# Output gates for all tokens ahead of the recurrence, and masked scores of two head parities in turn, in the mixer of a two-block network

## The chip, the cores and the metric

The kernel runs on one core of one Trainium2 chip. The metric is the device time of one execution, in microseconds (us), as the median of several runs; less is better. TensorE (PE) multiplies matrices, and its weight loads (PEld) overlap with its products; VectorE (DVE), ScalarE (ACT) and GpSimd (POOL) do the work by elements, and SyncE (SP) issues most of the DMA.

## The reference, cut to what matters

The network has two blocks over 512 tokens of 1024 features. The first is a gated layer, an attention and a second gated layer; the second is a token mixer and a channel mixer. The change lies in the token mixer. Half of its columns go through a convolution over 31 tokens, the other half through a recurrence of 8 heads of 64, with an output gate:

```python
p_rw = p_rw + (prev - p_rw) * rwkv_mu
r, k, v, wd, ad, gd = jnp.split(p_rw, RWKV_SPLITS, axis=-1)
a = jax.nn.sigmoid(a0 + ad @ a2)
g = jax.nn.sigmoid(gd) @ g2                     # gd has 160 columns, g 512
y = wkv7_scan(rh, heads(decay), kh, vh, kk, heads(a))
y = layer_norm(y, LNX_EPS).reshape(B, T, RWKV_WIDTH) * lnx_g + lnx_b
y = (y + bonus) * g
return jnp.concatenate([u, y], axis=-1) @ w_out
```

The recurrence is S = S * w - (S kk) (a kk)^T + v k^T, read with r at each token. All is float32.

## The kernel before, in words

Activations lie with features on the 128 partitions and tokens along the free axis. Large products split float32 operands into two parts that single passes carry; the small products of the mixer run on float32 as it is, and the trace records each of these as two halves, with a weight load for each.

The mixer (`mixer`, line 952) projects first. Column blocks of the second projection go in four groups (`PH`), and the small work that hangs on them is woven between: rates and gates of the decays beside group 1, the chain to the recurrence's matrices beside group 2 (`keynorm`, `decay`, `products`, `lower`, `bonus`), and the solve of 32 by 32 blocks on VectorE beside group 3 (`solve_step`, lines 1171 and 1174). The last blocks of group 3 are `d0` and `d1`, the 128 and the 32 columns of the gate's latent; `gd_done` shifts them (lines 1047, 1048) and takes their sigmoid on ScalarE (line 1233) into the tiles `gd0` and `gd1`.

Then `scan` (line 1257) runs the recurrence by 8 chunks of 64 tokens, in rounds of two chunks, i = 0 to 3. `prep(i)` makes ready what a round needs: `load` brings the solved blocks back from DRAM, `turn` transposes keys (line 1319), `scores(i, n)` for n = 0 to 3 makes masked products of heads (below), `inverse1` and `inverse2` finish the inverses. `seq(i)` is the chain from chunk to chunk: `step1`, `step2`, `step3`, each one or two groups of products on TensorE, then a copy on ScalarE (lines 1368, 1374) or a sum and a product on VectorE (lines 1388, 1391). `post(i)` reads the outputs of the round before: `read`, then `norm1`, `norm2`, and `norm3`, which applies norm, bonus and gate. The taps of the convolution (124 of them, line 1000, VectorE) fill VectorE's gaps; the first 70 may run before the solve is done. After the taps come the convolution's mean and norm (`conv_mean`, `conv_rstd`, `conv_out`), then the output's products.

`scores(i, n)` has one bank of PSUM and four products of 64 rows each. Heads of even number lie on partitions 0 to 63, odd ones on 64 to 127; n % 2 is the parity, so that one call uses one half of the array's rows. VectorE then multiplies the bank by the masks (line 1337).

`norm3(i)` multiplies, for its 128 tokens, the gate's latent by the four column blocks of `g2`: eight products of 128 columns into one bank, alternately 128 and 32 rows deep, and VectorE takes the gate from PSUM (line 1434). The two parts of `g2` are loaded on POOL's queue at the start of `scan` (lines 1266, 1267).

The order of the work is set twice. `weave` emits lists of (cost, step) at even progress of their costs. Then the framework's planner orders each engine's instructions by that order and by when its model has them ready, and gives out tiles and banks; on the chip each engine runs its queue in that order. The program has eight PSUM banks (`bank`).

Of the kernel before, what the change touches and what calls it, by code (L numbers as in the profile page):

```python
# [19 lines left out]
P = 128  # L20
# [10 lines left out]
# order of work where the blocks of a projection and what hangs on them share the engines  # L31
# of the latents (a, b: queries, c: keys and values, l: rotary key) with S: rstd by tokens,
# C: norm of c, N and R: norm and rotation of l
LATENTS = "cSclalNaCbbR"
HOLD = 3, 2  # steps of the last of the first projection's blocks that wait for the softmax; those of its first round
# column blocks of the second projection: the first six, then those beside the rates, the chain to the
# recurrence's matrices, and the solve; t: values turned
PH = "u0 g0 w u1 g1 k0", "k1 k2 k3 r0", "r1 r2 r3 u2 g2", "v0 v1 t0 v2 t1 v3 t2 u3 t3 g3 d0 d1"
W_IN2 = [n for p in PH for n in p.split() if n[0] != "t" and n != "d1"]
EARLY = 70  # taps of the convolution before the solve is done  # L40
CUT = 0, 24, 49, 74, 99, 124  # taps by stage of the recurrence
NE = 2  # column blocks of the output begun beside the recurrence
# steps between the output and the next projection, at each half block of the first and each K tile of the second
# [4 lines left out]
# ---------------------------------------------------------------- host layout  # L48
def _cols(v, n=None):
    """A vector as columns of 128 partitions, zero padded."""  # L50
    v = np.asarray(v).reshape(-1)
    k = -(-v.size // P)
    if v.size != k * P:
        v = np.concatenate([v, np.zeros(k * P - v.size, v.dtype)])
    return v.reshape(k, P).T


def _swapped(v):
    """The halves of the last axis swapped: what a rotation takes the sine of."""
    return np.roll(v, v.shape[-1] // 2, -1)  # L60


def _wtiles(w):
    """[K, M] -> [M/128, 128 (k in tile), K/128, 128 (m in tile)]."""
    k, m = w.shape
    return np.ascontiguousarray(w.reshape(k // P, P, m // P, P).transpose(2, 1, 0, 3))


def _narrow(w):
    """[K, 32] -> [128 (k in tile), K/128 * 32]."""  # L70
    return np.ascontiguousarray(w.reshape(-1, P, 32).transpose(1, 0, 2)).reshape(P, -1)
# [43 lines left out]
def _constants():  # L115
    """Matrices that depend on shapes alone."""
# [111 lines left out]
# ---------------------------------------------------------------- order of work  # L228
def pipe(n, *stages):
    """Stages (cost, f(u)) of n units, later stages of earlier units first."""  # L230
# [9 lines left out]
def weave(*streams):  # L240
    """Emits lists of (cost, f), each in its own order, all at even progress."""
# [13 lines left out]
# ---------------------------------------------------------------- program  # L255
class Net:
# [28 lines left out]
    # ---- small things  # L285
# [12 lines left out]
    @contextmanager  # L298
    def phase(self, name, third=True):
        """A pool for a part of the program; with room for a third block of weights or without."""  # L300
        with self.tc.tile_pool(name=name, bufs=1) as p:
            self.pt = p
            self.slots = self.slots[:2] + ([(p, 2)] if third else [])
            yield p
# [18 lines left out]
    # ---- exact halves of float32 operands  # L323
    def weights(self, src, n, keep=None):
        """A block of weights [128, n] in two parts that single passes carry."""
# [15 lines left out]
    def weights_at(self, src, n, at):  # L341
        """The same in two given tiles."""
# [21 lines left out]
    def dense(self, ps, src, x, m=P):  # L364
        """ps = W^T x over the K tiles of x, W's column block at src ([128, K/128 * 128])."""
# [3 lines left out]
    def dense_steps(self, bank, src, x, after=None, m=P, split=8):  # L369
        """The same in steps of `split` K tiles; after(ps) when it is done."""  # L370
# [19 lines left out]
    def narrow_steps(self, src, x, new, after, gain=None, m=P):  # L390
        """32 columns: a fourth of the K tiles in each fourth of the array's columns, then their sums in m rows,
        the columns and those with swapped halves in turn. x(k): the terms of a K tile; gain: per feature."""
# [27 lines left out]
    def dense_halves(self, src, x, last, done, mid):  # L420
        """A dense block by halves of the tokens; done(h, ps), and pieces of other work by K tile of the second."""
# [15 lines left out]
    def group_halves(self, src, n, x, room, side, ws=(), done=None, W=6):  # L437
        """group by halves of the tokens: weights (but ws, those of the first K tiles) stay in room(k); side: other work after the K tiles of both halves."""
# [24 lines left out]
    def group(self, src, n, x):  # L463
        """n column blocks at once, K tile by K tile: for operands that x(k) makes one by one."""
# [9 lines left out]
    # ---- norms over features (partitions)  # L474
    def add_square(self, acc, x, first, gain=1.0):
        """acc += (gain * x)^2"""
# [9 lines left out]
    def rstd(self, acc, mat, r, eps=1e-6, rows=P, last=None):  # L486
        """r = -1/sqrt(mat^T (acc + last) + eps); acc is used up."""
# [7 lines left out]
    def nrsqrt(self, r, v, t, eps):  # L495
        """r = -1/sqrt(v + eps), with a Newton step behind the tables; t is scratch."""
# [8 lines left out]
    def log_exp(self):  # L505
        """Ln and Exp from one table of ScalarE."""
        self.tc.keep_in_program_order(self.nc.scalar.preload_act_table_set("natural_log_exp_and_others"))

    def gained(self, k, g):
        """x[k] * gain per feature in two parts."""  # L510
# [7 lines left out]
    # ---- first block  # L518
    def warm(self):
        """Matmuls of zeros while the first loads are on their way: the tensor engine's clock rises with use."""  # L520
# [5 lines left out]
    def first(self, k):  # L526
        """Loads a tile of the input; its gains and squares."""
# [11 lines left out]
    def swiglu(self, acc, gname, gu, down, new2=None, side=((), (), ()), start=None):  # L539
        """x += half a gated layer; side: work for the gaps of the other engines, a piece a column block."""  # L540
# [73 lines left out]
    def entry(self, acc1, acc2):  # L614
        """What the mixer's input asks for; acc1 and acc2 are the sums of x^2 and (x g')^2."""
# [3 lines left out]
        # gains with the signs that the norms (all negative) ask for  # L619
# [9 lines left out]
    def enter(self, h, k):  # L629
        """A tile of the mixer's input in two parts, half h of the tokens: x g rr + shift; x, spilled, is used up.  # L630
        Of the final norm and the next, y = x rstd(x) g', then y rstd(y), both roots in one:
        rstd(x) rstd(y) = 1/sqrt(mean((x g')^2) + eps mean(x^2) + eps^2)."""
# [17 lines left out]
    def attention(self, acc):  # L650
        nc, A = self.nc, self.A
        new = self.acc()
        with self.phase("att", False) as pa:
# [26 lines left out]
            def norm_head(src, sq, gain, out, mat):  # L680
                """out = -src * gain / rms(src) over the groups of mat; sq holds src squared."""
# [9 lines left out]
            # latents and rotary key (r is negative, so are these before their norms)  # L691
# [42 lines left out]
            def b_keys(f):  # L734
                """Of heads 2 f and 2 f + 1."""
# [23 lines left out]
            def b_query_norm(h):  # L759
                """With the rotation's two terms one above the other: against the rotated key twice."""  # L760
# [69 lines left out]
            # softmax and values, head by head  # L830
# [6 lines left out]
            def scores(u):  # L837
# [4 lines left out]
                else:  # L842
                    q, k = qka[f][rows], qka[4 + f][rows]
                    # minus the bias: at [p, f] the one for q - k = p + 384 - f
# [18 lines left out]
            def transposes(u):  # L863
                pts[u] = [tile_([P, T], f"pt{4 * (u % 2) + j}") for j in range(4)]
                # key tile j of queries i >= j
# [6 lines left out]
            def values(u):  # L872
                """Of heads u and u + 1, side by side in the columns of the array."""
# [32 lines left out]
    # ---- second block  # L906
    def modulation(self):
        """mod = silu(c) W + b as 48 columns, in pieces for the gaps of another phase."""
# [24 lines left out]
        def total(g, part=(0, 1)):  # L933
            """Sums over partitions, side by side in the columns of the array: a quarter for half a group."""
# [6 lines left out]
        def fold(p):  # L941
            """The sums of two groups as columns, and their bias."""
# [19 lines left out]
    def mixer(self, acc1, acc2, stop):  # L962
# [17 lines left out]
        with self.phase("mix", False) as pa:  # L980
# [4 lines left out]
            gd = [keep([P, T], "gd0"), keep([32, T], "gd1")]  # L985
# [4 lines left out]
            def conv(j, t):  # L990
                """A tap of the convolution over tokens."""
# [12 lines left out]
            # ------------ projections  # L1004
# [12 lines left out]
            def room(n):  # L1017
                """Two tiles for a block of weights, in what the recurrence doesn't use yet or any more."""
# [16 lines left out]
            def residual():  # L1035
                """1/rms(x), spilled."""
# [4 lines left out]
            def shifted(j, out):  # L1041
                """out = p (1 - mu) + prev mu, tile j of the recurrent columns."""
# [26 lines left out]
            def rates(i):  # L1069
                """Decay rates, tokens on partitions."""  # L1070
# [12 lines left out]
            def keynorm(f):  # L1083
                """kk = k k_k / max(|k k_k|, 1e-12) over a head."""
# [12 lines left out]
            def decay(f):  # L1097
                """Decays within a chunk: up to t, up to t - 1, and back."""
# [30 lines left out]
            def lower(f):  # L1129
                """-L (rows t, columns s) of the 16 chunks of a head pair."""  # L1130
# [19 lines left out]
            def bonus_v(f):  # L1150
                """The bonus times v, when both are there."""
# [4 lines left out]
            def solve_start():  # L1156
                """(I - B)^-1 of 32 by 32 blocks, a block a partition."""
# [47 lines left out]
            def v_turn(f):  # L1205
                """Values with a chunk's tokens on partitions."""
# [29 lines left out]

            first()
# [14 lines left out]
            weave(D_(PH[3]), solve)  # L1252
            gains, scratch = (ncg, nlg, ngt, nfg), (dB, dT, dX, dY)
            return self.scan(tile_, xt_, room, ra, kb, bv, vt, gd, pcm, cv, convs, gains, scratch, stop)

    def scan(self, tile_, xt_, room, ra, kb, bv, vt, gd, pcm, cv, convs, gains, scratch, stop):
        """The recurrence by chunks of 64 tokens, its norms and gates, the convolution, the output."""
# [7 lines left out]
        masks, g2, g2b, cen = xt_(5), xt_(6), xt_(7), tile_([P, P], "tiny")  # L1265
        nc.gpsimd.dma_start(g2, A["g2"][:P])
        nc.gpsimd.dma_start(g2b[:32], A["g2"][P:])
# [13 lines left out]
        # ------------ norm of the convolution  # L1281
# [23 lines left out]
        # ------------ recurrence  # L1305
        def load(i):
            """Inverses of the blocks of 32: the first of a chunk as it is, both transposed."""
# [7 lines left out]
        def turn(c):  # L1315
            """Keys (both kinds, one above the other) of a chunk with tokens on partitions."""
# [8 lines left out]
        def scores(i, n):  # L1325
# [336 lines left out]
```

## Time and profile before

| | us |
|---|---|
| median of 3 runs | 1731.52 (1730.7 to 1740.45) |
| span of the profiled execution | 1719.0 |
| TensorE busy in it | 1682.8 (98%) |
| VectorE busy | 1025.7 (60%) |
| ScalarE busy | 715.3 (42%) |
| GpSimd busy | 51.4 (3%) |

The profile is of one execution. Its span goes from the first instruction to the last; the device time that the runs give has some us more around it, and of the profiled execution only the span is known. Times of rows count from the start of the span. The ends of TensorE's products are modelled, so durations of neighbouring products overlap by some 0.1 us; the time that a group takes is read from its start to the start of the next.

### The profile page before, as it was taken

The numbers are of one execution on the slowest core, as the hardware profiler recorded it, in microseconds if no ns is written. First come the engines' busy times: TensorE is split into PE (matmuls) and PEld (weight loads), VectorE is DVE, ScalarE is ACT, GpSimd is POOL, SyncE is SP. The second block draws the span as 40 slices with busy tenths as digits, with TensorE's granted clock in tenths as the row PEclk, the third lists the DMA queues.
The fourth block names the chain that finished last, engine by engine and source line by source line (L and its number), as shares of the span: only waits on it lengthen the run. The fifth ranks groups of instructions, "written<-read, shape, count | busy, mean of one in ns | idle before, by whom it ended". The sixth has DMA issues, their size and how long they took to land.

```text
span 1719.0 us, 21909 instructions
## 1 busy us (share of the span) xinstructions
PE 1682.8 (98%) x8644; PEld 1360.1 (79%) x8644; DVE 1025.7 (60%) x1706; ACT 715.3 (42%) x1163; POOL 51.4 (3%) x104
## 2 busy tenths in 40 slices
PE   9999999999999999999999999999999999999997
PEld 7888888877776788778877877787869988888886
DVE  4544434347788655754455469996777776666224
ACT  5422222247678352222222344632346554444222
POOL 0000000000000100100010000000000000000000
PEclk9999999999999999999999999996989999999998
DMA  5333333342111534753364332321033223333332
GB/s 176 99 97 94 94 95 99 98 133 88 56 55 38 178 92 147 243 174 99 98 220 145 115 103 62 98 67 41 5 105 96 75 77 98 98 99 93 91 101 83
DMA packets 63864, 177.17 MB, mean 103 GB/s; under 512 B 17066, under 2 KB 19370, under 8 KB 63761
## 3 DMA queue, kind: packets, MB, share of 16 engines
q1 hardware_dynamic: 52016, 138.96, 27.0%
q0 software_dynamic: 9872, 34.71, 6.4%
q10 hardware_dynamic: 1872, 2.10, 0.4%
q8 instruction: 68, 1.11, 0.3%
q14 instruction: 36, 0.29, 0.1%
HBM read 169.19 MB, written 6.55 MB: 102 GB/s over the span
## 4 chain that ended last, share of the span: by engine, by line
PE 78%; issue 7%; DVE 7%; DMA 6%; ACT 2%; DVEq 0%; POOL 0%; ACTq 0%; SPq 0%; POOLq 0%
PE ps L321 77%; DMA ada<-in_ada_w 5%; PE ps L869 1%; DVE adas L931 1%; DVE wlo L351 1%; DVE Ts L1174 0%; DVE Tm L1171 0%; DVE acc L484 0%; DVE f L1608 0%; DVE x L1514 0%; DVE x L1609 0%; DVE x L1515 0%; DMA raw<-in_w_in2k 0%; PE ps L1319 0%; DMA x<-in_x 0%
## 5 line engine op out<-in xcount | busy, mean ns | idle before, releaser
L350 ACT CAST whi<-raw 128x1024 fp32r<-128x1024 f32 (+1 forms) x244 | 248.9, 1020 | 584.5 <-PE ps L321 431.8
L351 DVE TENSOR_TENSOR wlo<-raw,whi 128x1024 fp32r<-128x1024 f32 (+1 forms) x244 | 289.1, 1185 | 256.2 <-ACT whi L350 246.6
L321 PE MATMUL ps<-xh,whi 128*128 128x512 f32 (+1 forms) x1008 | 401.0, 399 | 1.3 <-ACT xh L514 1.3
L321 PE MATMUL ps<-xh,wlo 128*128 128x512 f32 (+1 forms) x1008 | 392.1, 389 | 4.2 <-DVE wlo L351 4.2
L321 PE MATMUL ps<-xl,whi 128*128 128x512 f32 (+1 forms) x1008 | 391.5, 388 | 0.3 <-DVE xl L515 0.3
L321 PEld LDWEIGHTS ps<-xh,whi 128*128 128x128 f32 x1008 | 189.9, 189 | 50.6 <-issue 5.8
L321 PEld LDWEIGHTS ps<-xh,wlo 128*128 128x128 f32 x1008 | 189.4, 188 | 46.5 <-DVE wlo L351 6.8
L321 PEld LDWEIGHTS ps<-xl,whi 128*128 128x128 f32 x1008 | 189.7, 188 | 43.9 <-issue 5.3
L321 PE MATMUL ps<-hh,wlo 128*128 128x512 f32 (+1 forms) x560 | 211.5, 378 | 5.8 <-DVE wlo L351 5.8
L321 PE MATMUL ps<-hh,whi 128*128 128x512 f32 (+1 forms) x560 | 212.0, 379 | 0.0
L321 PE MATMUL ps<-hl,whi 128*128 128x512 f32 (+1 forms) x560 | 211.1, 377 | 0.0
L321 PE MATMUL ps<-oh,whi 128*128 128x512 f32 (+1 forms) x360 | 134.5, 375 | 0.0
L321 PE MATMUL ps<-ol,whi 128*128 128x512 f32 (+1 forms) x360 | 134.4, 374 | 0.0
L321 PE MATMUL ps<-oh,wlo 128*128 128x512 f32 (+1 forms) x360 | 134.4, 373 | 0.0
L321 PEld LDWEIGHTS ps<-hh,wlo 128*128 128x128 f32 x560 | 106.2, 190 | 26.6 <-DVE wlo L351 7.5
L321 PEld LDWEIGHTS ps<-hh,whi 128*128 128x128 f32 x560 | 106.2, 190 | 25.0 <-issue 5.9
L321 PEld LDWEIGHTS ps<-hl,whi 128*128 128x128 f32 x560 | 106.1, 190 | 19.4
L554 DVE TENSOR_TENSOR s<-s,ps 128x512 f32<-128x512 f32 x44 | 30.1, 687 | 109.8 <-PE ps L321 109.8
L552 DVE TENSOR_TENSOR s<-ps,r 128x512 f32<-128x512 f32 x44 | 30.2, 690 | 87.4 <-PE ps L321 87.4
L321 PEld LDWEIGHTS ps<-ol,whi 128*128 128x128 f32 x360 | 68.3, 190 | 11.9
L321 PEld LDWEIGHTS ps<-oh,wlo 128*128 128x128 f32 x360 | 68.2, 189 | 12.0
L321 PEld LDWEIGHTS ps<-oh,whi 128*128 128x128 f32 x360 | 68.1, 190 | 11.8
(457 smaller groups left out, 2227.6 us busy)
## 6 DMA issues: line engine op xcount, KB each, us to landing
raw<-in_ffn_gu SPq DMA_DIRECT2D x82, 512.0 KB, 3.6
ada<-in_ada_w POOLq DMA_DIRECT2D x48, 512.0 KB, 4.6
raw<-in_up SPq DMA_DIRECT2D x38, 512.0 KB, 3.6
raw<-in_ffn_d SPq DMA_DIRECT2D x32, 512.0 KB, 3.6
raw<-in_w_in SPq DMA_DIRECT2D x27, 512.0 KB, 3.6
raw<-in_w_out SPq DMA_DIRECT2D x16, 512.0 KB, 3.8
raw<-in_down SPq DMA_DIRECT2D x16, 512.0 KB, 3.5
raw<-in_ffn_d SPq DMA_DIRECT2D x16, 384.0 KB, 3.2
```

The source lines that it names most:

```text
L321: self.nc.tensor.matmul(*a, **k)
L350: nc.scalar.copy(hi[:, :n], raw[:, :n])
L351: nc.vector.tensor_sub(lo[:, :n], raw[:, :n], hi[:, :n].bitcast(F32))
L552: nc.vector.tensor_mul(s, pg, r)
L554: nc.vector.tensor_mul(s, s, pu)
L869: nc.tensor.transpose(ps[:, i * P : (i + 1) * P], es[u, i][:, j * P : (j + 1) * P], self.c("ident"))
L931: nc.vector.scalar_tensor_tensor(st[g][q], h, sc[:, k : k + 1], st[g][q], op0=ALU.mult, op1=ALU.add)
```

## The change

The gate's products for all tokens move from `norm3` to the end of the projections: `gate_load` loads `g2` before group 3, and four steps `gate(f)`, woven behind group 3, make two products of 512 columns each into four banks. After the fourth, ScalarE copies the four banks into the tiles that held `g2` and the latent. `norm3` has no products any more and takes the gate from these tiles in SBUF; its cost for `weave` falls from 1.8 to 0.1.

`scores(i, g)` now makes two parities at once, with a bank for each, and issues their products in turn; both masks follow. Two calls of cost 1.8 replace four of 0.9.

Comments and docstrings are removed too.

```diff
-            gd = [keep([P, T], "gd0"), keep([32, T], "gd1")]
+            gd, gt = [keep([P, T], "gd0"), keep([P, T], "gd1")[:32]], []
...
+            def gate_load():
+                st["g2"] = xt_(6), xt_(7)
+                nc.gpsimd.dma_start(st["g2"][0], A["g2"][:P])
+                nc.gpsimd.dma_start(st["g2"][1][:32], A["g2"][P:])
+
+            def gate(f):
+                fs, (g2, g2b) = slice(f * P, (f + 1) * P), st["g2"]
+                st["gate", f] = ps = self.bank()
+                self.mm(ps, g2[:, fs], gd[0], start=True, stop=False)
+                self.mm(ps, g2b[:32, fs], gd[1], start=False, stop=True)
+                if f == 3:
+                    gt.extend((xt_(6), xt_(7), keep([P, T], "gd0"), keep([P, T], "gd1")))
+                    for n, t in enumerate(gt):
+                        nc.scalar.copy(t, st["gate", n])
...
-            weave(D_(PH[3]), solve)
+            gate_load()
+            weave(D_(PH[3]) + sum([item(1.7, gate, f) for f in range(4)], []), solve)
...
-        masks, g2, g2b, cen = xt_(5), xt_(6), xt_(7), tile_([P, P], "tiny")
-        nc.gpsimd.dma_start(g2, A["g2"][:P])
-        nc.gpsimd.dma_start(g2b[:32], A["g2"][P:])
+        masks, cen = xt_(5), tile_([P, P], "tiny")
...
-        def scores(i, n):
-            ps = self.bank()
-            sc = tile_([P, T], (f"s{i % 2}", f"s{2 + i % 2}", "di", "kk")[n], bufs=(1, 1, 2, 2)[n])
+        def scores(i, g):
+            ps, sc = [], []
+            for n in (2 * g, 2 * g + 1):
+                ps.append(self.bank())
+                sc.append(tile_([P, T], (f"s{i % 2}", f"s{2 + i % 2}", "di", "kk")[n], bufs=(1, 1, 2, 2)[n]))
             for m in range(2):
-                h = n % 2 + 4 * (n // 2) + 2 * m
-                f, R = h // 2, HR(h)
                 for q in range(2):
                     ct, k = slice(i * P + q * 64, i * P + q * 64 + 64), 2 * m + q
-                    o = ps[:, k * P : (k + 1) * P].rearrange("p (n t) -> p n t", n=2)
-                    self.mm(o, kb[f][R, 2 * i + q].rearrange("p n t -> p (n t)"), ra[f][R, :, ct], start=True, stop=True)
-                    st["sc", 2 * i + q, h] = sc[:, k * P : (k + 1) * P]
-            nc.vector.tensor_mul(sc, ps, masks)
+                    for n in range(2):
+                        h = n + 4 * g + 2 * m
+                        f, R = h // 2, HR(h)
+                        o = ps[n][:, k * P : (k + 1) * P].rearrange("p (n t) -> p n t", n=2)
+                        self.mm(o, kb[f][R, 2 * i + q].rearrange("p n t -> p (n t)"), ra[f][R, :, ct], start=True, stop=True)
+                        st["sc", 2 * i + q, h] = sc[n][:, k * P : (k + 1) * P]
+            for n in range(2):
+                nc.vector.tensor_mul(sc[n], ps[n], masks)
...
         def norm3(i):
             y4, ti = st["y", i], slice(i * P, (i + 1) * P)
-            pg = self.bank()
             for f in range(4):
-                fs = slice(f * P, (f + 1) * P)
-                self.mm(pg[:, fs], g2[:, fs], gd[0][:, ti], start=True, stop=False)
-                self.mm(pg[:, fs], g2b[:32, fs], gd[1][:, ti], start=False, stop=True)
-            for f in range(4):
-                fs, y = slice(f * P, (f + 1) * P), y4[:, f, :]
+                y = y4[:, f, :]
                 nc.vector.scalar_tensor_tensor(y, y, nlg[:, f : f + 1], bv[f][:, ti], op0=ALU.mult, op1=ALU.add)
-                nc.vector.scalar_tensor_tensor(y, y, self.v("lnxb", f), pg[:, fs], op0=ALU.add, op1=ALU.mult)
+                nc.vector.scalar_tensor_tensor(y, y, self.v("lnxb", f), gt[f][:, ti], op0=ALU.add, op1=ALU.mult)
                 self.halves(os_[4 + f][0][:, ti], os_[4 + f][1][:, ti], y)
...
-            + sum([item(0.9, scores, i, n) for n in range(4)], []) + item(1.7, inverse1, i) + item(1.7, inverse2, i)
+            + sum([item(1.8, scores, i, g) for g in range(2)], []) + item(1.7, inverse1, i) + item(1.7, inverse2, i)
...
-            item(1.7, read, 2 * i) + item(1.7, read, 2 * i + 1) + item(0.9, norm1, i) + item(0.9, norm2, i) + item(1.8, norm3, i)
+            item(1.7, read, 2 * i) + item(1.7, read, 2 * i + 1) + item(0.9, norm1, i) + item(0.9, norm2, i) + item(0.1, norm3, i)
```

## Rows read from the trace of the kernel before

**Rows 1.** The page: busy time by engine; the chain that ended last, by engine.

```profile
PE 1682.8 (98%) x8644; PEld 1360.1 (79%) x8644; DVE 1025.7 (60%) x1706; ACT 715.3 (42%) x1163; POOL 51.4 (3%) x104
...
PE 78%; issue 7%; DVE 7%; DMA 6%; ACT 2%; DVEq 0%; POOL 0%; ACTq 0%; SPq 0%; POOLq 0%
```

**Rows 2.** Stretches: length, busy us and instructions by engine; granted clock, DMA share, GB/s.

```profile
1164.00:1174.10 10.10, 6.53 (x78) 4.91 (x74) 9.60 (x21) 6.51 (x8) 0.00 (x0) 1.00 0.41 126
1174.10:1204.80 30.70, 30.64 (x238) 27.91 (x239) 15.39 (x24) 5.24 (x10) 0.00 (x0) 0.50 0.09 15
...
1225.30:1228.60 3.30, 3.30 (x18) 2.97 (x19) 2.65 (x5) 0.56 (x1) 0.00 (x0) 0.50 0.00 0
...
1249.20:1255.90 6.70, 6.70 (x74) 6.29 (x71) 4.99 (x12) 0.04 (x1) 0.00 (x0) 0.50 0.30 82
...
1273.10:1279.80 6.70, 6.70 (x39) 4.06 (x40) 3.01 (x11) 1.07 (x4) 1.06 (x2) 0.50 0.35 116
...
1204.80:1275.60 70.80, 69.94 (x764) 57.23 (x763) 51.84 (x95) 25.91 (x49) 2.69 (x5) 0.91 0.17 52
```

**Rows 3.** The chain in order of time: start us, us, what.

```profile
1228.00 27.84 PE ps L321 x324
...
1281.47 0.70 DVE acc L1287
...
1297.64 22.40 PE ps L321 x165
```

**Rows 4.** Timeline of TensorE, gate products and what follows: start us, us, operation.

```profile
1220.70 3.40 PE L321 MATMUL ps<-gd,x 128*128 128x128 f32 x16
1224.03 1.19 PE L321 MATMUL ps<-dpm,rf 32*32 32x32 f32 x32
...
1270.08 3.68 PE L321 MATMUL ps<-gd,x 128*128 128x128 f32 x16
1273.69 0.49 PE L321 MATMUL ps<-s,vt 128*64 128x64 f32 x4
```

**Rows 5.** Timeline of TensorE, fp32 products of 512 columns and what follows.

```profile
1284.69 3.79 PE L321 MATMUL ps<-sq,cst 128*128 128x512 f32 x8
1288.32 3.29 PE L321 MATMUL ps<-gd,x 128*128 128x128 f32 x16
```

**Rows 6.** Waits of TensorE, 1164 to 1304: us in total, times, longest.

```profile
PE ps L321 <- ACT oh L355: 3.3, 2, 2.6
PE ps L321 <- DMA dpm<-dT: 1.7, 1, 1.7
```

**Rows 7.** Groups of VectorE, 1166 to 1305: busy us, mean ns, idle before.

```profile
L1434 DVE SCALAR_TENSOR_TENSOR B<-B,vec,ps 128x128 f32<-128x128 f32 x16 | 5.1, 343 | 0.0
L1433 DVE SCALAR_TENSOR_TENSOR B<-B,col,bv 128x128 f32<-128x128 f32 x16 | 5.1, 347 | 0.0
```

**Rows 8.** Timeline of ScalarE: the gate's second sigmoid.

```profile
1169.59 0.62 ACT L1233 ACTIVATE gd<-gd 32x512 f32<-32x512 f32 x1
```

**Rows 9.** Timeline of POOL: the second load of g2.

```profile
1112.02 0.51 POOL L1267 DMA_DIRECT2D x<-in_g  x1 [3.94 <-DVE x L1123]
```

**Rows 10.** Timeline of TensorE: masked scores (ra,kb), and what follows two of them.

```profile
1166.76 2.82 PE L321 MATMUL ps<-ra,kb 64*128 64x128 f32 x32
...
1180.11 3.09 PE L321 MATMUL ps<-ra,kb 64*128 64x128 f32 x16
...
1185.03 2.07 PE L321 MATMUL ps<-ra,kb 64*128 64x128 f32 x8
...
1207.74 1.17 PE L321 MATMUL ps<-ra,kb 64*128 64x128 f32 x12
1208.84 1.14 PE L321 MATMUL ps<-x,dpm 64*64 64x64 f32 x16
...
1211.05 1.16 PE L321 MATMUL ps<-ra,kb 64*128 64x128 f32 x8
1212.13 1.16 PE L321 MATMUL ps<-vt,kbt 128*128 128x128 f32 x8
```

More of the change, by code (lines that the diff above doesn't have):

```diff
@@ L1251, in mixer, with scan @@
             weave(D_(PH[2]), chain)
-            weave(D_(PH[3]), solve)
+            gate_load()
+            weave(D_(PH[3]) + sum([item(1.7, gate, f) for f in range(4)], []), solve)
             gains, scratch = (ncg, nlg, ngt, nfg), (dB, dT, dX, dY)
-            return self.scan(tile_, xt_, room, ra, kb, bv, vt, gd, pcm, cv, convs, gains, scratch, stop)
-    def scan(self, tile_, xt_, room, ra, kb, bv, vt, gd, pcm, cv, convs, gains, scratch, stop):
+            return self.scan(tile_, xt_, room, ra, kb, bv, vt, gt, pcm, cv, convs, gains, scratch, stop)
+    def scan(self, tile_, xt_, room, ra, kb, bv, vt, gt, pcm, cv, convs, gains, scratch, stop):
         nc, A = self.nc, self.A
```

## The prediction

> **What bounds the kernel now.** I read the page first: TensorE is busy in 98% of the span and carries 78% of the chain that ended last [rows 1]. A microsecond saved there counts, if TensorE is also what ends the waits where it is saved. The change touches one stage, from the end of the second projection (1164 us) to the start of the output (1304 us). Its stretches come next [rows 2]: TensorE is busy without a gap from 1174.1 and nearly so to 1275.6, VectorE for half to three quarters of that, ScalarE and the DMA little. The second thing to see there is the granted clock: 0.50 (1.2 GHz) from 1174.1 to 1204.8, then full (2.4 GHz) but for three falls of 3.3 to 6.7 us before 1280. Third, the chain of waits [rows 3]: TensorE's products alone carry it to 1256 and, behind a weight block, to 1281.5; from there to 1297.6 it is VectorE and ScalarE, the convolution's norm, and TensorE has room beside it.
>
> **Gate products taken out of norm3.** One norm3 runs 8 fp32 products of 128 columns, recorded as 16 halves: from 1220.70 to the next product at 1224.03, 3.33 us; the third time, 1270.08 to 1273.69, 3.61 [rows 4]. There are four; the second repeats the first. Three lie before 1275 on the path: 3.33 + 3.33 + 3.61 = 10.3 us go. The fourth, at 1288.32 [rows 5], lies beside the convolution's chain, and TensorE waits behind it anyway (2.6 us until 1297.64) [rows 3, 6]: I count it at nothing; that chain is the cover, without it 3.3 us more would go. VectorE's sixteen products by the gate read SBUF instead of PSUM: the same form with all its tensors in SBUF takes 347 ns against 343 [rows 7], nothing.
>
> **Gate products added ahead of the recurrence.** Eight products of 512 columns, 16 halves. The nearest row is the convolution's norm: 8 fp32 halves of 512 columns from 1284.69 to the next product at 1288.32, 0.454 us each [rows 5], so 16 x 0.454 = 7.3 us. What lies beside it: half of the gate's latent is ready only when ScalarE's sigmoid ends at 1170.21 [rows 8]. Between 1164 and 1174.1 TensorE is busy 6.53 of 10.10 us [rows 2]; the 3.6 idle are waits for copies, masks and, the longest (1.7), for the solved blocks by DMA [rows 6]. Ready work can fill them: 7.3 - 3.6 = 3.7 us are added. The ends: 0, if the products displace later idle time too, and 7.3, if all run ahead of the inverses that could start at 1171. ScalarE's four copies (some 0.6 each, by the 128x512 sigmoid's kind of size [rows 8], 2.4 us) fall into stretches in which it is busy 6.51 of 10.10 and 5.24 of 30.70 us [rows 2]: nothing; ahead of the copy between the inverses they would cost 2.4. The two loads of g2 move forward on POOL's queue. The second went out at 1112.02 already, after a wait for the tile that VectorE frees [rows 9]; that is 52 us before they are needed now, and what stands behind them, masks and zeros, is needed in the recurrence: nothing. If they landed late, all of the 7.3 would be on the path, the upper end above.
>
> The Trainium skill says under Key Properties of "TensorEngine Tiling (Array Packing)" that a change of tiling mode drains TensorE. The old gate products alternate between 128 and 32 rows, and their halves take 0.208 us (3.33 / 16), where eight halves of the state's update, all of 128 rows, show 1.16 us, 0.145 each [rows 4, 10]. By that rule the new ones, eight products at twice the difference, would cost 8.3 instead of 7.3. The trace has the price for 128 columns only, and the sum stays with 7.3.
>
> **Masked scores of the two parities in turn.** One parity is four products, 8 halves, on 64 rows of the array. Alone it takes 1.08 us (1211.05 to 1212.13) at the full clock and 2.0 at half (1185.03, with 0.07 of modelled end) [rows 10]. Where two parities follow each other with nothing between, they run side by side: 12 halves, 4 of one parity and 8 of the next, from 1207.74 to 1208.84, 1.10 us, no longer than 8 alone [rows 10]. In turn, each pair should cost one, 1.1 us. Round 0: 32 halves in 2.8 us become 2.2, but behind them TensorE waits for the DMA: hidden. Round 1, at half clock: 3.0 for a pair in a row and twice 2.0 become 2 x 2.0, saves 3.0. Rounds 2 and 3: two parities alone (1.08 each), then 0.6 for half a parity by the row of 8, and the 1.10, in all 3.9; with 2.2 each saves 1.7. Sum 3.0 + 1.7 + 1.7 = 6.4. The ends: 0, if they don't run side by side; 8, if the two pairs of a round follow each other and overlap too. The first parity's mask now waits for both, up to 1 us; the inverses need all four masks, so no one waits for that one.
>
> **The clock.** The three falls between 1204.8 and 1280 each come within 5 us of a gate product's start (1220.7 and 1225.3; 1270.1 and 1273.1; the second repeats them) [rows 2, 4], which streams at two thirds of the rate of its neighbours. Without them I expect these falls to go: half clock for 3.3 + 6.7 us and 2.5 up to 1275.6 gives back half, 6.3 us (ends 0 and 6.3). The long one, 30.7 us, came behind the 3.6 us of idle time. With wide products in that place and the scores paired, part of it should go, between 0 and 15.3 us, half of 30.7. I take 5, a third, since the inverses on 32 rows that stood around the fall remain.
>
> **What is late next.** From 1204.8 to 1275.6 VectorE is busy 51.84 of 70.8 us [rows 2]; TensorE's part shrinks to 70.8 - 10.3 - 3.4 - 6.3 = 50.8. Two engines equally full that wait for each other don't both run without gaps. The ends: 0 us lost, if VectorE's remaining taps move into the first stretch (busy 15.39 of 30.70), and 20, if VectorE stays at today's share of 73%, which keeps the 70.8. I take 7, a third, nearer to the lower end because the taps are free to move.
>
> **Sum.** -10.3 + 3.7 - 6.4 - 6.3 - 5 + 7 = -17.3 us. The profiled span is 1719.0; the median of the three runs is 1731.52, 12.5 more, which I take as what lies around the span and leave as it is. After 1304 TensorE is the chain again [rows 3], and its weights' rooms come free from the recurrence itself, so the gain is kept: 1731.5 - 17.3 = 1714.2, say **1714**.
>
> **Rivals.** *The clock holds through the recurrence.* For it: paired scores fill both halves of the array, and the wide products stream without a break. Against: the inverses and the waits around them stay. The other 10 us of the first stretch come back: 1704. Chance 0.15.
>
> *TensorE was the cover, not the bound.* VectorE ends last nearly everywhere, 14 instead of 7 us are lost, and in the waits the clock falls as before (of the 6.3 half): about 1714 + 7 + 3 = 1724. For it: 51.8 us against 50.8. Against: from 1204.8 to 1275.6 TensorE is busy 69.94 of 70.8 us [rows 2]. Chance 0.27.
>
> *The pairs don't run side by side*, or the order of the queue parts them: the 6.4 stay, 1720.5. Against: the 12 halves. Chance 0.07.
>
> *Slower.* The gate products stand in TensorE's queue ahead of the inverses and wait there for the sigmoid, and they hold four of the program's eight banks until the last is copied, so that transposes and scores wait for banks. All from 1171 on is late by 7.3 and the 1.7 waited, 9 us. It decides if the recurrence is bound by the chain from chunk to chunk and not by TensorE, so that none of the 10.3 and 6.4 comes back; with the half clock some 10 us longer, 5 more: 1745. Chance 0.05. The Trainium skill points this way under Gotcha 1 of "TensorEngine Tiling (Array Packing)": row tiles raise the pressure on PSUM, as each needs a bank of its own. No row of before shows a wait for a bank.
>
> **How the numbers follow.** The forecast has 0.46, with a range of its own from 1706 to 1721. A measurement of this kernel can tell about 1%, 17.3 us, and the forecast lies on that line (1714.2): half of its chance (0.23) is faster, half the same. The clock's case is all faster (0.15), and so is a quarter of the lost cover's and of the pairs' (0.09). Faster 0.47, same 0.49, slower 0.04, nearly all of the last case. The range goes from 1700 (the clock's case and 4 us) to 1729 (the lost cover with 5 us more of the gate products on the path).
>
> **What would show it.** Right: no product of the gate's latent after 1185; 16 halves of 512 columns before, near 7.3 us in all; scores of 16 halves in 1.1 us; the full clock from about 1200 to the convolution's mean; waits of TensorE for ScalarE and VectorE in the recurrence, some 7 us in all. Wrong: the falls of the clock where they were, without the gate products; gate products that wait for the sigmoid with the inverses behind them; a stage that ends at 1304 as before.

## The result and the profile after

The changed kernel takes 1707.33 us (median of 4 executions, 1705.04 to 1709.47) where the kernel before, run beside it, takes 1731.11 (4 executions, 1722.40 to 1740.45): ratio 0.9854, interval [0.9814, 0.9893]. The forecast was 1714, range 1700 to 1729. In later runs, with more executions (12 and 30), it was 1706.91 against 1716.83: 0.9943 [0.9922, 0.9965]. Six of the 63 later executions of the kernel before were in a slower state: they count in its medians, but not in the ratios and the clock columns below. The changed kernel takes the same both times, the kernel before does not, and how far the runs explain this is the main thing to learn here.

The page of the changed kernel, as in [rows 1]: the span, TensorE's busy time, and the chain's shares by engine.

```profile
span 1706.2 us, 21821 instructions
PE 1662.1 (97%) x8596; PEld 1340.5 (79%) x8596; DVE 1025.2 (60%) x1706; ACT 717.3 (42%) x1167; POOL 51.4 (3%) x104
...
PE 76%; DVE 8%; issue 7%; DMA 7%; ACT 2%; POOL 0%; DVEq 0%; ACTq 0%; SPq 0%; POOLq 0%
```

This execution took 1708.19, so only 2.0 us lie around its span, and 1.7 to 2.2 in the executions below. The profiled execution of before (span 1719.0) therefore took about 1721, like the shortest of its four. The two traces differ by 12.8 us, half of what the medians of these first runs do.

To see where, I cut the stage at the same work in both kernels: the end of the latents, the first inverse, the second, fourth and last update of the state (the last cut is the convolution's mean), and the eighth load of the next projection's weights. First the kernel before, then the changed one; the busy times are those of TensorE, its weight loads, VectorE, ScalarE and POOL.

```profile
core 0: us, PE busy (x) PEld busy (x) DVE busy (x) ACT busy (x) POOL busy (x), PEclk, DMA share, GB/s
1163.50:1171.30 7.80, 5.42 (x52) 3.69 (x44) 7.23 (x19) 5.91 (x8) 0.00 (x0) 1.00 0.40 143
1171.30:1200.40 29.10, 27.85 (x249) 25.06 (x249) 14.56 (x23) 4.86 (x9) 0.00 (x0) 0.55 0.13 20
1200.40:1225.10 24.70, 24.70 (x270) 20.49 (x268) 17.09 (x26) 7.98 (x14) 0.00 (x0) 0.91 0.05 8
1225.10:1249.90 24.80, 24.80 (x285) 20.48 (x282) 17.36 (x33) 8.29 (x17) 1.09 (x2) 0.92 0.06 22
1249.90:1275.70 25.80, 24.94 (x239) 20.38 (x237) 21.01 (x41) 10.81 (x19) 1.60 (x3) 0.83 0.36 113
1275.70:1339.90 64.20, 60.72 (x421) 52.38 (x421) 46.91 (x96) 42.66 (x88) 2.13 (x4) 0.91 0.31 93
```

```profile
1162.30:1177.00 14.70, 12.14 (x66) 5.70 (x58) 14.15 (x29) 8.77 (x12) 0.00 (x0) 1.00 0.35 98
1177.00:1200.20 23.20, 20.16 (x245) 18.13 (x246) 16.34 (x26) 4.65 (x8) 0.00 (x0) 0.71 0.05 8
1200.20:1218.50 18.30, 17.63 (x261) 15.23 (x259) 16.62 (x26) 5.83 (x11) 0.00 (x0) 1.00 0.09 14
1218.50:1240.30 21.80, 20.18 (x265) 16.60 (x264) 15.05 (x31) 8.38 (x17) 1.09 (x2) 0.89 0.08 25
1240.30:1263.20 22.90, 20.63 (x189) 17.28 (x188) 12.78 (x24) 9.96 (x18) 1.60 (x3) 0.81 0.34 107
1263.20:1326.90 63.70, 57.51 (x436) 49.98 (x435) 48.69 (x102) 44.82 (x92) 2.13 (x4) 0.95 0.31 102
```

Read the first number behind the times, row by row. The start is 6.9 us longer, the stretch of the first inverses 5.9 shorter with its mean clock up from 0.55 to 0.71, the next three shorter by 6.4, 3.0 and 2.9. Busy time times PEclk is roughly TensorE's work at the full clock: in those three rows it falls from 22.5 to 17.6, 22.8 to 18.0 and 20.7 to 16.7, while its idle time rises from 0.0, 0.0 and 0.9 to 0.7, 1.6 and 2.3.

The start in the timeline of TensorE (start, duration, the wait ahead and its releaser in brackets), the rows that answer to [rows 4, 5, 10]:

```profile
1163.77 1.04 PE L321 MATMUL ps<-sq,cst 128*32 128x512 f32 x2 [0.71 <-ACT sq L411]
1164.74 3.70 PE L321 MATMUL ps<-gd,x 128*128 128x512 f32 x8
1169.19 3.69 PE L321 MATMUL ps<-gd,x 32*128 32x512 f32 x8 [0.74 <-ACT gd L1233]
1172.81 1.09 PE L1334 MATMUL ps<-cst,kb 128*128 128x128 f32 x8
1173.84 2.06 PE L321 MATMUL ps<-ra,kb 64*128 64x128 f32 x32
1177.12 0.22 PE L321 MATMUL ps<-dpm,s 32*32 32x32 f32 x2 [1.23 <-ACT kbt L1338]
```

The gate products are one block of 8.1 us, and transposes, scores and inverses all stand behind it. The wait of 1.23 us is put down to ScalarE's copy of the keys (`kbt`), but that copy had ended 0.74 us before. What ended just before the first inverse began, at about 1177.0, was VectorE's first mask, and more waits for masks follow:

```profile
1175.31 1.07 ACT L1338 COPY kbt<-ps 128x512 f32<-128x512 f32 x2
1176.35 1.27 DVE L1357 TENSOR_TENSOR s<-ps,x 128x512 f32<-128x512 f32 x2
...
1178.93 0.24 PE L321 MATMUL ps<-dpm,di 32*32 32x32 f32 x2 [0.89 <-DVE di L1357]
1179.53 0.24 PE L321 MATMUL ps<-dpm,kk 32*32 32x32 f32 x2 [0.35 <-DVE kk L1357]
```

The falls of the clock from there on, in the same columns as above:

```profile
1180.70:1194.40 13.70, 12.65 (x106) 11.51 (x108) 7.63 (x13) 2.65 (x5) 0.00 (x0) 0.51 0.07 11
1235.40:1242.20 6.80, 6.80 (x57) 5.43 (x55) 0.68 (x1) 2.04 (x4) 1.09 (x2) 0.51 0.25 78
1249.00:1255.80 6.80, 6.45 (x39) 5.50 (x38) 2.53 (x6) 1.02 (x3) 0.00 (x0) 0.51 0.45 153
1286.60:1293.40 6.80, 5.65 (x26) 5.65 (x27) 6.80 (x19) 5.97 (x12) 0.00 (x0) 0.51 0.00 0
```

The long one is 13.7 us instead of 30.7 [rows 2], but two more stand in the recurrence, with no gate product near. Last, TensorE's waits from 1155 to 1290 (total us, times, longest), which answer to [rows 6]:

```profile
PE ps L321 <- ACT oh L355: 4.6, 2, 2.7
PE ps L321 <- ACT sq L1309: 1.8, 1, 1.8
PE ps L321 <- ACT vt L1394: 1.7, 3, 0.7
PE ps L321 <- ACT kbt L1338: 1.2, 1, 1.2
```

The 2.7 us under `oh` are not new: it is the wait of 2.6 us in front of the output's products [rows 6], which ends at 1297.64 in the kernel before and at 1287.75 here. Ahead of that wait, the largest entry of before is the DMA of the solved blocks, 1.7 us, and no other is over 0.7. Here there are 1.9 us for a cast near 1247, 1.8 for a square of the convolution's norm, 1.7 for copies in the chain from chunk to chunk, and the waits for masks: ScalarE and VectorE now end more of TensorE's waits.

### The profile page after: what moved, and what is told of

Its sections match the earlier page's. It is cut to its first block, busy times and chain, and to the rows that moved or that the text cites. A ratio compares the mean times of both kernels' runs of the same rounds, so it can differ in the third digit from the quotient of the medians.

```text
span 1706.2 us, 21821 instructions
## 1 busy us (share of the span) xinstructions
PE 1662.1 (97%) x8596; PEld 1340.5 (79%) x8596; DVE 1025.2 (60%) x1706; ACT 717.3 (42%) x1167; POOL 51.4 (3%) x104
## 4 chain that ended last, share of the span: by engine, by line
PE 76%; DVE 8%; issue 7%; DMA 7%; ACT 2%; POOL 0%; DVEq 0%; ACTq 0%; SPq 0%; POOLq 0%
PE ps L321 75%; DMA ada<-in_ada_w 5%; PE ps L869 1%; DVE adas L931 1%; DVE wlo L351 1%; DVE Ts L1174 0%; DVE Tm L1171 0%; DVE acc L484 0%; DMA raw<-in_w_out 0%; DVE f L1623 0%; DVE x L1529 0%; DVE x L1000 0%; DVE x L1624 0%; DVE x L1530 0%; DMA raw<-in_w_in2k 0%
```

## The experiments

For each execution the runs list the span and its mean granted clock. I take 2 x (1 - clock) x span as its time at half clock. Over 145 executions of the kernel before and the ten runs below, taken within each kernel, one microsecond more at half clock goes with 0.40 us more span. (That it is less than half fits TensorE's waits in such stretches, 5.65 of 6.80 us busy in the last row of the falls above.) So "span less 0.4 x half-clock time" compares kernels roughly as if the clock were the same; the clock is recorded to three digits, so one half-clock time goes in steps of 3.4 us. The ratios are against the kernel before, run beside them; a1 to e3 are one chip, r3 to x4 a second, y1 and y2 a third.

| run | median us | ratio, interval | at half clock, median (range) | span less 0.4 of it |
|---|---|---|---|---|
| before (with a1 to e3) | 1716.83 | 1 | 68.6 (58 to 104) | 1687.4 |
| a1_after | 1706.91 | 0.9943 [0.9922, 0.9965] | 51.1 (44 to 75) | 1685.5 |
| e1_gates_only | 1718.59 | 0.9997 [0.9976, 1.0019] | 67.0 (55 to 72) | 1690.0 |
| e2_scores_only | 1720.35 | 1.0003 [0.9974, 1.0032] | 80.8 (48 to 93) | 1686.4 |
| e3_gates_woven | 1700.78 | 0.9897 [0.9861, 0.9933] | 32.2 (20 to 58) | 1685.7 |
| before (with r3 to x4) | 1718.24 | 1 | 72.0 (58 to 107) | 1687.0 |
| r3_gates_woven | 1697.74 | 0.9899 [0.9875, 0.9924] | 28.8 (24 to 58) | 1683.8 |
| x1_spare_products | 1709.71 | 0.9951 [0.9929, 0.9972] | 30.7 (27 to 51) | 1692.9 |
| x2_woven_by_parity | 1702.88 | 0.9921 [0.9901, 0.9940] | 30.6 (30.6 to 40.9) | 1688.9 |
| x4_gates_ahead | 1714.40 | 0.9957 [0.9925, 0.9990] | 65.2 (34 to 79) | 1685.7 |
| y1_early_behind | 1694.65 | 0.9864 [0.9822, 0.9906] | 28.8 (20 to 37) | 1681.0 |
| y2_early_split | 1693.03 | 0.9873 [0.9823, 0.9922] | 27.1 (17 to 61) | 1680.3 |

**The changed kernel again** (no edit).

> The changed kernel again, unchanged, beside the three below on one chip. If the gain is work of TensorE (theory), the ratio to the kernel before comes out again near 0.986 and the span is again 1706 within 3 us, and the falls of the granted clock after 1230 stand behind the same waits (the early output blocks' casts near 1247, the convolution's norm). If the falls are chance (rival), they stand elsewhere, and the span of this profile may be some 5 us off.

It is 9.9 us faster than before, not 23.8. 17.5 us less at half clock make 7.0 of them, and the last column gives 1.9; differences of medians need not add up, and 1.0 is left. Its profiled execution shows the swing within one kernel: span 1714.5, since the clock fell earlier and for longer than in the first trace.

```profile
1168.70:1175.50 6.80, 6.80 (x30) 4.25 (x30) 5.17 (x8) 4.02 (x6) 0.00 (x0) 0.51 0.27 43
1178.90:1213.00 34.10, 32.76 (x296) 30.00 (x297) 20.99 (x33) 6.22 (x11) 0.00 (x0) 0.50 0.05 9
```

The expected ratio missed its mark, and so did the span, by 8 us; at 0.40 the clock (0.978 against 0.986) accounts for more than that. On the first two falls after 1230 the theory held and the rival did not: in both traces one comes behind the same two waits in the chain from chunk to chunk (0.96 and 0.67 us; falls at 1235.4 and 1243.8), the next behind the wait for the early output blocks' cast (1.91 and 1.68 us; falls at 1249.0 and 1257.5). A third fall, 3.4 us from 1278.0, is new. What differed most was the stretch at the start.

**The gate products alone**, and **the paired scores alone**. The first is the changed kernel with the old `scores`; the second the old kernel with

```diff
-            + sum([item(0.9, scores, i, n) for n in range(4)], [])
+            + sum([item(1.8, scores, i, g) for g in range(2)], [])
```

and the new `scores`.

> Only the gate products move; the masked scores are issued by parity as before. Theory (TensorE bounds the recurrence, and the two parts add up): three products in norm3 go (-10.3), about 6 come back at the start, and part of the first low stretch of the clock goes (-8): about 12 us faster than before, and 6 slower than the changed kernel, the terms of the pairs. Rival 1 (the gain is the clock at the start alone, which the wide products keep up): within 2 us of the changed kernel. Rival 2 (VectorE bounds the stage and TensorE was cover): either nearly all of the gain or nearly none, and the scores alone the other.

> Only the scores are paired; the gate products stay in norm3. Theory: 3.0 + 1.7 + 1.7 = 6.4 us of TensorE go, 16 halves take 1.1 to 1.2 us at the full clock and 2.0 to 2.2 at half, and about 5 to 7 us of the time go. The falls of the clock near the gate products (1225, 1273) stay if those products cause them, and go if they don't. Rival 1 (clock at the start): the long low stretch is as long as before, 30 us, and the time within 2 us of before. Rival 2 (VectorE): within 2 us of before, with TensorE's waits for VectorE and ScalarE longer by what the pairs save.

Neither part alone gains anything, so neither the sum of my terms nor the gates' rival 2 (one part alone gives all) holds. The trace of the gates alone, cut as above:

```profile
1163.90:1181.20 17.30, 15.83 (x66) 8.85 (x58) 14.80 (x29) 8.80 (x12) 0.00 (x0) 0.80 0.30 84
1181.20:1209.90 28.70, 27.46 (x250) 24.84 (x249) 14.77 (x23) 4.65 (x8) 0.00 (x0) 0.55 0.05 8
1209.90:1231.30 21.40, 21.40 (x257) 18.72 (x256) 15.95 (x25) 5.82 (x11) 0.00 (x0) 0.89 0.06 10
1231.30:1251.10 19.80, 19.80 (x265) 17.03 (x264) 16.18 (x34) 8.16 (x17) 1.09 (x2) 1.00 0.01 3
1251.10:1273.50 22.40, 20.05 (x189) 16.53 (x188) 14.01 (x26) 9.96 (x18) 1.60 (x3) 0.85 0.41 132
```

Against before, the three stretches of the recurrence are shorter by 3.3, 5.0 and 3.4, in all 11.7 us: the products taken out of norm3 do come back. The start is 9.5 longer, partly at half clock, and takes nearly all of it. With the pairs alone, 16 halves do take what was expected, and the half-clock time is 12 us longer, not shorter; at equal clock they give 1.0:

```profile
1195.49 1.16 PE L321 MATMUL ps<-ra,kb 64*128 64x128 f32 x16
```

Here rival 2 came out nearly as it was put: the ratio is 1.0003, and between the outer cuts (1159.4 to 1335.3) TensorE's idle time is 14.1 us against 8.0 before, 6.1 more where 6.4 were to be saved; the waits that grew are mostly for ScalarE. And the falls stayed near the gate products: at 1212.4, 1236.3 and 1263.6, behind gate products that start at 1207.36, 1232.39 and 1262.16. In the gates alone, without these products, the clock falls in the recurrence only once behind the long stretch (1259.0).

**The gate products woven between the inverses.**

```diff
-            weave(D_(PH[3]) + sum([item(1.7, gate, f) for f in range(4)], []), solve)
+            weave(D_(PH[3]), solve)
...
-        weave(prep(0), cut(0))
+        g_ = lambda f: item(1.7, gate, f)
+        prep0 = (
+            item(0.1, load, 0) + item(0.4, turn, 0) + item(0.4, turn, 1) + item(1.8, scores, 0, 0) + item(1.8, scores, 0, 1)
+            + g_(0) + g_(1) + item(1.7, inverse1, 0) + g_(2) + item(1.7, inverse2, 0) + g_(3)
+        )
+        weave(prep0, cut(0))
```

> The gate products are issued behind the first chunk's transposes and scores: two column blocks ahead of the first inverse, one between the two, one behind. Theory (the block of 8 us at the start holds up transposes, scores and inverses by 6 us while ready work of the same queue could fill those waits): first inverse 2 to 4 us sooner than in the changed kernel, products beside the waits for copies, 2 to 5 us faster than the changed kernel. Rival 1 (clock): the low clock comes some 5 us sooner and stays longer, since the idle time ahead of the inverses is back or the products run at half clock, 0.9 us a half; no gain or up to 8 us slower than the changed kernel.

It beats both kernels: 16.1 us under before and 6.1 under the changed one, and on the second chip (r3) 20.5 under before. TensorE's timeline (waits in brackets):

```profile
1163.56 2.06 PE L321 MATMUL ps<-ra,kb 64*128 64x128 f32 x32
1165.54 1.12 PE L321 MATMUL ps<-gd,x 128*128 128x512 f32 x2
1167.12 3.23 PE L321 MATMUL ps<-gd,x 32*128 32x512 f32 x6 [0.45 <-ACT gd L1233]
1170.28 0.43 PE L321 MATMUL ps<-dpm,s 32*32 32x32 f32 x8
...
1171.40 2.18 PE L321 MATMUL ps<-gd,x 128*128 128x512 f32 x4
1173.51 1.19 PE L321 MATMUL ps<-dpm,rf 32*32 32x32 f32 x32
1174.63 2.18 PE L321 MATMUL ps<-gd,x 128*128 128x512 f32 x4
```

The first inverse starts 10.0 us after the end of the latents instead of 14.7, and the waits for the masks and for the copy between the inverses are full of products. Cut as before, the stretch from there to the second update has no time at half clock:

```profile
1170.30:1189.40 19.10, 18.43 (x258) 14.19 (x257) 18.03 (x28) 6.58 (x12) 0.00 (x0) 1.00 0.14 23
```

This is not so in every execution. In the profile of r3, the same kernel, the clock fell at 1170.5, ahead of the two later groups of gate products, which then take twice as long, and stayed low for 23.9 us (the first of them in the timeline, then the stretch):

```profile
1172.76 4.08 PE L321 MATMUL ps<-gd,x 128*128 128x512 f32 x4
```

```profile
1170.50:1194.40 23.90, 23.23 (x149) 15.58 (x150) 13.81 (x22) 5.03 (x9) 0.00 (x0) 0.50 0.10 16
```

That execution had 58 us at half clock; of the six of each chip, one had 58 and the others 20 to 37. So the woven products make the time at half clock shorter in most executions, and do not rule the long stretch out.

Did the order help, or the clock? Both stood in the expectation's theory, so three more runs part them.

**Only work added to the kernel before**: the same products at these places, their banks read by no one. Norm3 keeps its own.

```diff
+        def spare(f):
+            fs, ps = slice(f * P, (f + 1) * P), self.bank()
+            self.mm(ps, g2[:, fs], gd[0], start=True, stop=False)
+            self.mm(ps, g2b[:32, fs], gd[1], start=False, stop=True)
...
+            + g_(0) + g_(1) + item(1.7, inverse1, 0) + g_(2) + item(1.7, inverse2, 0) + g_(3)
```

> The kernel before, and in it the eight 512-column gate products (7.3 us) issued a second time, unread, between the first chunk's scores and inverses as in the woven kernel; norm3 keeps its own gate products and the scores stay by parity. So only work is added. Theory C (the time follows the granted clock, and products between the inverses keep it up): time at half clock falls from some 69 us to 35 to 50, and the kernel is 5 to 12 us faster than before although it does more. Rival W (what counts is the work that TensorE is spared): 3 to 7 us slower than before.

Work was added and the kernel became 8.5 us faster: theory C holds, and the rival is out by its sign. The half-clock time falls by 41 us (worth 16.5), and the last column rises by 5.9 for the added products. In the trace, from the end of the latents to the eighth load:

```profile
1161.40:1326.20 164.80, 157.24 (x1518) 127.90 (x1511) 124.82 (x236) 79.90 (x154) 4.82 (x9) 0.96 0.24 69
```

TensorE's work (busy x PEclk) is 151 where the rows of before sum to 142; the stretch is 11.6 us shorter at a clock of 0.96.

**The woven kernel with the scores by parity.** The edit is the old `scores` and its four items.

> The woven kernel with the masked scores by parity as before, so without the second part of the change. Theory W (TensorE's work counts): 6.4 us slower than the woven kernel. Theory C (in the recurrence at the full clock what the pairs save becomes waits for ScalarE and VectorE): within 3 us of the woven kernel if the time at half clock is within 5 us of its, and else slower by 0.4 of the difference in that time.

By medians it is 5.1 us slower than the woven kernel beside it, at nearly the same half-clock time (30.6 against 28.8), and 5.1 by the last column too; by the means of the last column (1688.0 and 1684.2) it is 3.8. That lies between C's 3 and W's 6.4. With 5 and 6 executions, whose intervals of the ratio overlap, no more than this is shown: while the clock is kept, TensorE's work does count, likely at more than half.

**All gate products ahead of both inverses**, but behind the scores.

```diff
-            + g_(0) + g_(1) + item(1.7, inverse1, 0) + g_(2) + item(1.7, inverse2, 0) + g_(3)
+            + g_(0) + g_(1) + g_(2) + g_(3) + item(1.7, inverse1, 0) + item(1.7, inverse2, 0)
```

> The woven kernel with all four blocks of gate products behind the scores but ahead of both inverses, none between or behind them. Two reasons are told apart for what weaving gained over the changed kernel. Theory C (the products between the inverses fill the waits for their copies, and the clock stays up): the long stretch at half clock of 13 to 34 us behind the inverses is back, and the kernel is 4 to 8 us slower than the woven one, near the changed one. Rival H (the block no longer holds up transposes and scores): as fast as the woven kernel within 2 us.

16.7 us slower than the woven kernel, twice what C expected, and by its ratio level with the changed one: H is out. The wait between the inverses is back, and the clock falls behind it (the timeline, then the stretch):

```profile
1175.51 0.41 PE L321 MATMUL ps<-dpm,s 32*32 32x32 f32 x8
...
1176.84 1.19 PE L321 MATMUL ps<-dpm,rf 32*32 32x32 f32 x32 [0.67 <-ACT rf L1367]
```

```profile
1177.80:1218.80 41.00, 39.66 (x324) 35.64 (x322) 23.22 (x37) 6.77 (x12) 0.00 (x0) 0.50 0.05 8
```

At equal clock (last column) it stands at 1685.7, within 2 us of the woven kernel. So the place of the products acts mainly through the clock.

**The early output blocks moved.** y1, on top of the woven kernel; y2 puts the second block beside the convolution's norm.

```diff
-        weave(seq(3), post(2), early)
+        weave(seq(3), post(2) + early)
```

> The woven kernel with the two early output blocks issued behind the third chunk pair's reads and norms instead of woven among them. In the woven kernel their first product waits 2.0 us for a cast on ScalarE near 1235 and holds TensorE's queue, and the clock falls 2 us later. Theory (such waits are what the freed time went into, and they call the fall behind them): 2 to 5 us faster than the woven kernel. Rival (VectorE or the chain of chunks bounds this stretch, and TensorE's wait only moves): within 1.5 us of the woven kernel, the wait found again in front of the state's products.

> The same, with one of the two early output blocks there and the other beside the convolution's norm, where TensorE waits 2.3 us for a square on ScalarE near 1256. Theory: both waits shrink, 3 to 6 us faster than the woven kernel and the falls behind 1237 and 1258 gone or shorter. Rival: within 1.5 us of the woven kernel.

By medians y1 and y2 are 3.1 and 4.7 us under the woven kernel on the second chip (r3), at about the same time at half clock; the intervals of the ratios overlap, so the gain is likely and not established. In y1's profile the 2.0 us wait is gone, but waits of 2.3 us for the copies of step 1 and of 2.7 for the squares of the outputs' norm have come in. The falls near 1237 and 1258 are still there (1237.6 and 1258.1, 3.4 us each, as in the woven kernel), so these runs do not show that the wait called the fall behind it. In y2's profile the long stretch at the start is at half clock, as in r3's. These are the shortest medians of the study, 1.4% and 1.3% under the kernel before.

## Why the prediction came out right

The time was inside the range, and that was in part luck: wrong terms and a base that was read wrongly offset each other. The sum was -17.3 us; the traces show -12.8 and the later runs -9.9, and with the later median of before, 1716.8, the same sum would have given 1699.5, under the range.

- **Base.** I put 12.5 us around the span, and there are 2.0. Against the profiled execution of about 1721, the sum of -17.3 would have given 1704, and its trace showed -12.8. The 10 us more that I added came back as the kernel before's own swing, between 55 and 107 us at half clock in the later runs. The clocks of the kernel before's first executions are not recorded, so that its 1731 has the same cause is likely, not shown.
- **Gate products out of norm3, -10.3.** Right: in the gates alone the three stretches are 11.7 us shorter, and by busy time times PEclk, which leaves the clock out, 10.1; no product of the latent stands behind 1173.
- **Gate products added, +3.7.** This is the step that failed. "Ready work can fill" the 3.6 idle us: it could not, because turns and scores, which had filled part of that time, went behind the block, and the block waited 0.74 us for the sigmoid with all of them queued. The start grew by 6.9 us in the first trace and by 9.5 in the gates alone, 3.4 of which are half of the 6.8 us at half clock: 6.1 to 6.9, near the upper end of 7.3. Woven, half of the products lies behind the first inverse, and the start is 10.0 us, 2.2 longer than before.
- **Their price.** 16 halves took 7.3 us grouped by depth (the block of 8.07 less its wait of 0.74), as in the sum. Where they alternate between 128 and 32 rows, 16 halves of the spare products took 8.4 (1167.49 to 1171.70 for eight, and twice 2.10 for the others). The Trainium skill's rule that a change of tiling mode drains TensorE ("TensorEngine Tiling (Array Packing)", Key Properties) agrees with this: the estimate by it was 8.3. No row shows the drain itself. (The estimate took the 128-row halves at 0.145 us with their modelled end; from start to next start, 1212.13 to 1213.22, they are 0.136, which makes it 8.4.)
- **Scores, -6.4.** The form was right: 16 halves in 1.16 us at the full clock, 2.08 at half. Their worth was some 4 to 5 us with the clock kept up, 1.0 alone. "No one waits" for the masks that now stand behind both parities was wrong: ahead of and among the first inverses TensorE waited 1.23, 0.33, 0.89 and 0.35 us for them, where the gates alone, by parity, show 0.22 and 0.35.
- **The clock, -6.3 and -5.** Wrong in both places. Falls come without the gate products, at 1235 and 1249, though with the products in place, in the pairs alone, each stood within 5 us of one: whether these products call a fall stays open. And the long one is not shorter by a set share: it took 13.7 us in one execution of the changed kernel, 6.8 and 34.1 in another. Together the two terms were 11.3 us, and the 12 executions show 7.0.
- **Lost cover, +7.** Near in size, but not in place: TensorE's idle time between the outer cuts rose from 8.0 us to 16.4, but in the three stretches of the recurrence only from 0.9 to 4.6; the rest is among the first inverses and behind the convolution's mean.
- **Rivals.** That TensorE was cover is half true: its work at full clock fell by some 9 us (142 to 133 between the outer cuts), and at equal clock 2 us of time came of it. "The clock holds through the recurrence" did not happen in the changed kernel; it nearly did in the woven one's first trace (1.00 in the first inverses, then 0.92, 1.00 and 0.92 in the three stretches of the recurrence, with two short falls of 3.4 us near 1190 and 1237), whose medians are 1698 to 1701.

Open: why the half-clock time falls with both parts together (51 us) and with neither alone (67 and 81). The runs show it; nothing here shows the cause. Open too is why the same kernel on the same chip has the long fall in one execution and not in the next.

## What to carry to other kernels

When work is moved off a chain, look at what it stands in front of: as one block the same products held up all that was queued behind them for 6 to 7 us, and the gaps between the small products stayed empty. Look at the mean clock of each execution before you believe in a difference of a few microseconds, and compare kernels at equal time at half clock. Stretches of small products with short waits are where wide products, even useless ones, may pay; measure that over many executions, since a single profile can show the opposite.

## What had not been expected of the hardware

TensorE's clock falls to 1.2 GHz in stretches where the engine is recorded as busy all but 3% of the time (39.66 of 41.0 us), behind 32-row products and a wait of 0.67 us, and stays there for 41 us. Eight wide products around those inverses make it less frequent: 19.90 of 19.90 us busy at 1.00 in the kernel with spare products, where the kernel before had 27.85 of 29.10 at 0.55, and 30.7 against 72.0 us at half clock by the medians. They do not prevent it: with the same products the clock fell at the first inverse in r3 and y2, for 23.9 us. And one program on one chip swings by some 20 us from execution to execution with the time at half clock.
